# Inputs laid out by copies in a two-layer trunk kernel: x also transposed, weights in streaming order, state tables on their partitions, the scan in contiguous fours

## The chip, the cores and the metric

The kernel runs on one core of one Trainium2 chip. The metric is device time of one execution in microseconds (us), lower is better; the host's work on the inputs is outside it. PE is the matrix engine, DVE the vector engine, ACT the scalar engine, POOL the general one; SP issues most DMAs.

## The reference

Two layers run one after the other on x of 256 positions by 2048 features, fp32. Cut to what matters:

```python
for l in range(2):
    h = rmsnorm(x, pre_norm_g[l])
    q, k, v, z_att, u, z_ssm = split(h @ w_in[l])        # 2048 x 6144, 1024 columns each
    o_att = diff_attention(q, k, v, lam, rel_bias)       # 8 heads, softmax(q1 k1) - lam softmax(q2 k2), masked by chunks of 64
    o_att = rmsnorm(o_att, subln_g[l]) * (1 - lam_init) * silu(z_att)
    y = s5_ssm(u, a, dt, B, C, d)   # 64 groups of 16 channels: h[t] = abar h[t-1] + Bbar u[t], y = Re(C h) + d u
    g_val, g_gate = split(gelu(y) @ w_glu[l])            # 1024 x 2048
    o_ssm = g_val * sigmoid(g_gate) * silu(z_ssm)
    x = x + rmsnorm(concat(o_att, o_ssm) @ w_out[l], post_norm_g[l])   # 2048 x 2048
```

Everything must come out in fp32 accuracy.

## The kernel before, in words

**Halves.** Each layer's weights are cut into 72 chunks of 1 MB, each in two halves of 512 KB: 144 halves a layer, numbered `hs` from 0 (below "half 12" is `hs` = 12, "half 84" is `hs` = 84). A half comes by one DMA from SP's queue into `raw` (128 x 1024, five buffers). ACT copies it to `hi`, rounded to fp32r; DVE makes `lo = raw - hi`; PE multiplies hi by hi, hi by lo and lo by hi and so gets near-fp32 products. In halves 0 to 47 of a layer (U4, u, q, k) that is 24 multiplies of 256 columns; in 48 to 143 (v, za, zs, glu, out) 12 of 512 columns. The first eight halves (U4) fill four accumulators at once, later ones one or two. PSUM has four buffers for accumulators (`acc`) and four for everything else (`side`).

**Order.** The program is written out half by half in the loop over `hs`: DMA for half `hs` + 6, the end of the chunk before (`evac`), `hi` for `hs` + 2, then the other jobs that are due (generators started at fixed halves by `hooks`), `lo` for `hs` + 2, the half's multiplies (`main`), then side jobs that need PE (`run_second`). Each engine takes its own instructions in this order. Long DVE work, as the state scan, is cut into steps and filled in around `lo` by a budget (`fill`, `emit_lo`, constants `BUDS`, `SC`, `CAP`; `cost` is the planned time of a step):

```python
        load[0] += 68 + n / 0.96
            bal = min(bal, CAP) + (BUDL if not l and s >= 44 else BUDS[l]) + pload[0] - load[0] - 1130
```

**The head.** x is loaded by rows of positions (`load_x`, four column blocks of 512 KB between the first weight halves). `build` turns 128 x 128 pieces over PE (`psx`), then ACT writes `hthi` and DVE `htlo`: the transposed, scaled x in hi and lo parts, two of its 16 k pieces per half. `rstd_gen` sums squares on ACT, DVE makes 1/rms, PE spreads it over partitions (`psr`) and ACT copies it to `rbc`; the accumulators of U4 and u can only be read (`u = ac * rbc`, in `evac`) after that. `params_gen` transposes the state poles and vectors over PE and multiplies out the bias table (`psp`).

**State tables and scan.** `prep_gen` loads B and C of a layer by twelve DMAs whose rows are 16 elements long and transposes C over PE (`psc`, four runs of four); for layer 1 that happens in halves 96 onward of layer 0, beside glu. `s_gen` makes the inputs of the state by products (`pss`) and writes `H` (2 parts x 32 group pairs x 64 blocks of four positions). `scan_ops` then steps over the 62 later blocks, each four DVE instructions on 64 elements with a stride of 64. `y_gen` makes y from H (`psy`, `psz`), applies gelu on ACT and DVE, transposes it (`psg`) and writes `ghi` and `glo`, the inputs of glu, with elements 16 bytes apart. Attention runs per head as `soft_gen` (logits, softmax on ACT) and `pv_gen` (transposes `pwt`, ACT copies `wt`, PE makes `po`), in halves 51 to 90.

## Time and profile before

| | us |
|---|---|
| median of 3 runs | 926.35 (925.54 to 928.47) |
| the profiled execution | 926.7 |
| its span (first to last instruction) | 924.9 |
| PE / DVE / ACT busy in it | 907.7 / 683.5 / 488.1 |

The span is what the trace covers; 1.8 us of the execution lie around it. Busy times of the engines overlap, so they don't add up; PE's matmuls are pipelined, and a start-to-start distance says more of PE's pace than the length of one.

### The profile page before, as it was taken

What the parts mean: (1) busy time and instruction counts of PE and PEld (TensorE: products, weight loads), DVE (VectorE), ACT (ScalarE), POOL (GpSimd) and SP (SyncE); (2) the same over time, 40 slices, a digit from 0 to 9 for tenths busy, and PEclk for the clock granted to TensorE, in tenths of its full rate; (3) what the DMA queues carried; (4) which work ended last, traced back from release to release, by engine and by line L of the source; (5) the groups of instructions that cost most, each with busy time, mean ns of one, the idle gap of its engine ahead of it and who ended that gap; (6) DMA issues with size and microseconds to landing.
All of it is one profiled execution on the core that took longest, in us unless ns stands there. A gap on an engine that the chain in (4) does not pass through costs nothing.

```text
span 924.9 us, 17644 instructions
## 1 busy us (share of the span) xinstructions
PE 907.7 (98%) x6722; PEld 795.1 (86%) x6722; DVE 683.5 (74%) x1606; ACT 488.1 (53%) x881; POOL 17.2 (2%) x26
## 2 busy tenths in 40 slices
PE   9999999999999999999999999999999999999995
PEld 8999999888888788887889999997888788888884
DVE  4898686999995756877877449999966566665564
ACT  6643384455465667444468443335565655644451
POOL 3000000000000000000000000000000000000001
PEclk9999999999999999999999999999999999999998
DMA  9988656855654497576656866965556346665852
GB/s 303 209 231 244 185 165 172 278 158 168 184 155 137 126 232 243 171 249 201 215 173 193 230 175 168 246 187 165 163 156 183 115 137 203 197 210 168 291 183 91
DMA packets 187892, 177.21 MB, mean 192 GB/s; under 512 B 42550, under 2 KB 131184, under 8 KB 186912
## 3 DMA queue, kind: packets, MB, share of 16 engines
q1 hardware_dynamic: 187456, 175.96, 64.3%
q8 instruction: 53, 0.87, 0.4%
q14 instruction: 31, 0.25, 0.1%
q0 software_dynamic: 352, 0.13, 0.1%
HBM read 168.44 MB, written 7.88 MB: 191 GB/s over the span
## 4 chain that ended last, share of the span: by engine, by line
PE 87%; DVE 5%; ACT 3%; DMA 2%; SPq 1%; issue 1%; DVEq 0%; ACTq 0%
PE ac L113 79%; DVE lo L116 2%; DMA xt<-in_x_dram 1%; PE lga L113 1%; PE psy L113 1%; PE pss L113 1%; PE po L113 1%; SPq L496 1%; PE psw L97 1%; PE acu L113 1%; ACT junk L134 1%; DMA raw<-in_w_glu_dram 1%; ACT hi L134 1%; DMA raw<-in_w_in_dram 1%; ACT y L134 0%
## 5 line engine op out<-in xcount | busy, mean ns | idle before, releaser
L134 ACT ACTIVATE hi<-raw 128x1024 fp32r<-128x1024 f32 (+1 forms) x282 | 297.8, 1056 | 357.3 <-PE ac L113 272.2
L116 DVE TENSOR_TENSOR lo<-raw,hi 128x512 fp32r<-128x512 f32 (+1 forms) x401 | 359.8, 901 | 105.5 <-ACT hi L134 104.3
L113 PE MATMUL ac<-hthi,hi 128*128 128x256 f32 x736 | 211.7, 288 | 0.3 <-ACT hi L134 0.3
L113 PE MATMUL ac<-htlo,hi 128*128 128x256 f32 x736 | 209.4, 285 | 0.8 <-DVE htlo L123 0.5
L113 PE MATMUL ac<-hthi,lo 128*128 128x256 f32 x736 | 209.1, 284 | 0.6 <-DVE lo L116 0.5
L113 PE MATMUL ac<-hi,hthi 128*128 128x512 f32 x384 | 154.4, 402 | 0.0
L113 PE MATMUL ac<-lo,hthi 128*128 128x512 f32 x384 | 149.8, 390 | 0.4 <-DVE lo L116 0.4
L113 PE MATMUL ac<-hi,htlo 128*128 128x512 f32 x384 | 150.1, 391 | 0.0
L113 PEld LDWEIGHTS ac<-htlo,hi 128*128 128x128 f32 x736 | 141.8, 193 | 1.7 <-DVE htlo L123 1.7
L113 PEld LDWEIGHTS ac<-hthi,hi 128*128 128x128 f32 x736 | 141.7, 193 | 1.3 <-ACT hi L134 0.5
L113 PEld LDWEIGHTS ac<-hthi,lo 128*128 128x128 f32 x736 | 141.7, 193 | 1.2 <-DVE lo L116 1.2
L113 PE MATMUL ac<-lo,mxhi 128*128 128x512 f32 x228 | 89.0, 390 | 0.7 <-DVE lo L116 0.6
L113 PE MATMUL ac<-hi,mxhi 128*128 128x512 f32 x228 | 89.0, 391 | 0.0
L113 PE MATMUL ac<-hi,mxlo 128*128 128x512 f32 x228 | 88.7, 389 | 0.0
L113 PEld LDWEIGHTS ac<-hi,hthi 128*128 128x128 f32 x384 | 72.1, 188 | 16.1
L113 PEld LDWEIGHTS ac<-hi,htlo 128*128 128x128 f32 x384 | 72.1, 188 | 15.8
L113 PEld LDWEIGHTS ac<-lo,hthi 128*128 128x128 f32 x384 | 72.2, 188 | 14.6 <-DVE lo L116 0.8
L113 PEld LDWEIGHTS ac<-lo,mxhi 128*128 128x128 f32 x228 | 42.8, 188 | 10.3 <-DVE lo L116 1.5
L113 PE MATMUL ac<-hi,ghi 128*128 128x512 f32 x128 | 51.5, 403 | 0.0
L113 PEld LDWEIGHTS ac<-hi,mxlo 128*128 128x128 f32 x228 | 42.8, 188 | 8.9
L113 PE MATMUL ac<-lo,ghi 128*128 128x512 f32 x128 | 50.1, 391 | 0.3 <-DVE lo L116 0.3
L113 PEld LDWEIGHTS ac<-hi,mxhi 128*128 128x128 f32 x228 | 42.8, 188 | 8.9
(206 smaller groups left out, 1154.5 us busy)
## 6 DMA issues: line engine op xcount, KB each, us to landing
raw<-in_w_in_dram SPq DMA_DIRECT2D x191, 512.0 KB, 4.2
raw<-in_w_out_dram SPq DMA_DIRECT2D x64, 512.0 KB, 4.7
raw<-in_w_glu_dram SPq DMA_DIRECT2D x32, 512.0 KB, 4.3
U<-uds SPq DMA_DIRECT2D x48, 64.0 KB, 3.3
xt<-in_x_dram SPq DMA_DIRECT2D x8, 256.0 KB, 7.6
uds<-u SPq DMA_DIRECT2D x4, 512.0 KB, 6.0
pg<-in_post_norm_g_dram SPq DMA_DIRECT2D x2, 1024.0 KB, 7.1
xt<-in_x_dram SPq DMA_DIRECT2D x2, 1024.0 KB, 10.1
```

Of the source, the lines that this page charges most:

```text
L97: P.transpose(o, i, idn)
L113: P.matmul(o, lhsT=l, rhs=r, start=start, stop=stop, skip_group_check=True)
L116: V.tensor_tensor(o, a, b, op=op)
L134: A.activation(out=o, in_=i, func=f, **kw)
L496: SY.dma_start(out=bv[64 * d:64 * d + 64, a, r::2], in_=src[l].rearrange("(m r g) p c -> r g p m c", r=2, g=2)[r, d ^ r])
```

## The change

The host now hands over copies of the inputs in other layouts: `xt`, x transposed (x itself is still read for the residual); `wst`, the weights as 288 blocks of 128 x 1024 in the order in which they stream, so that a half is 128 rows of 4 KB in place of pieces of 512 or 2048 bytes; `vecs`, `poles`, `lams` and `bc`, the vectors, poles and B and C of the states already on the partitions on which the kernel uses them. In the kernel:

- The transposes of x in layer 0, of the poles and vectors, and of C in both layers go (`build0` reads `xT`). In layer 1, x is still transposed. The first two pieces of x^T are issued from ACT, the rest from SP between the weights.
- Squares of x in layer 0 are summed over k by DVE and over partitions by two small products (`psv`); `rstd_gen` starts at half 3, before at 1.
- B and C come by two DMAs of 512 KB.
- The scan takes the 64 blocks as 16 groups of four. H's last index is now 16*i + k (block i of group k). 24 steps of 1024 elements and 60 of 64 replace 248 of 64, in each layer; the 1024-wide ones read and write runs of 16 adjacent elements. `u`, `ghi` and `glo` change their order to match.
- `lo` is no longer cut in two around filled work; the budgets are changed; loads and stores of u move by two or three halves; the scan is put on the list before U's second load.
- A second u chunk gets a side buffer as accumulator; half 0 is written by pieces of k.

```diff
-SC = 70
+SC = 57
...
-CAP = 1500.0
-RES = 0.0
+CAP = 1800.0
...
-        load[0] += 68 + n / 0.96
-        return 68 + n / 0.96
+        load[0] += 147 + n / 0.955
+        return 147 + n / 0.955
...
     def emit_dma(hs):
         if hs >= 2 * NCH:
             return
-        l, seg, b = chunks[hs // 2]
...
-        else:
-            SY.dma_start(out=tv, in_=src)
+        SY.dma_start(out=t, in_=wst[hs])
...
         if (weave and budget > 0) or urgent:
             budget = UB if urgent else budget
-            fill(budget / 3)
-            for p in range(2):
-                c = slice(512 * p, 512 * p + 512)
-                tt(lo[:, c], src[:, c], hf[:, c], ALU.subtract)
-                fill(budget / 3)
+            fill(budget / 2)
+            tt(lo, src, hf, ALU.subtract)
+            fill(budget / 2)
...
         ps = side("psp")
-        tpose(ps[:, 0:128], pt[:, 128:256], ident)
-        tpose(ps[:, 128:192], pt[0:64, 384:512], ident[0:64, 0:64])
-        mm4(ps[0:8, 192:512], bt[0:32, 384:392], bt[0:32, 0:320], True, True)
+        mm4(ps[0:8, 0:320], bt[0:32, 384:392], bt[0:32, 0:320], True, True)
         ps2 = side("psp2")
         mm4(ps2[0:8, 0:64], bt[0:32, 384:392], bt[0:32, 320:384], True, True)
-        tpose(ps2[:, 64:82], bt[0:18, 1408:1536], ident[0:18, 0:18])
...
-        cn = R(cslot, "cn")
         cm = R(4, "cm")
         G.memset(cm, 0.0)
+        for c in range(2):
+            SY.dma_start(out=bt[:, 1024 * c:1024 * c + 1024], in_=bc[l, :, 1024 * c:1024 * c + 1024])
         bv = bt[:, 0:1024].rearrange("p (a m c) -> p a m c", a=2, m=NPAIR)
-        for a, src in enumerate((ssm_b_re, ssm_b_im)):
-            for d in range(2):
-                for r in range(2):
-                    SY.dma_start(out=bv[64 * d:64 * d + 64, a, r::2],
-                                 in_=src[l].rearrange("(m r g) p c -> r g p m c", r=2, g=2)[r, d ^ r])
...
         for a in range(2):
-            for hb in range(2):
-                yield 1
-                ps = side("psc")
-                for j in range(4):
-                    tpose(ps[:, 128 * j:128 * j + 128], cv[:, a, 4 * hb + j], ident)
...
-                    act(cmk[rows, 8 * hb:8 * hb + 8, put], pick, AF.Copy, scale=1.0 if a == 0 else -1.0)
-                    act(ccv[rows, a, 16 * hb:16 * hb + 16].rearrange("p (i r) c -> p i r c", r=2), pick, AF.Copy)
+            for d in range(2):
+                rows = slice(64 * d, 64 * d + 64)
+                put = slice(2 * a + 1, 2 * a + 5, 3) if d else slice(2 * a, 2 * a + 6, 5)
+                act(cmk[rows, :, put], ccv[rows, a].rearrange("p (i r) c -> p i r c", r=2), AF.Copy,
+                    scale=1.0 if a == 0 else -1.0)
...
+    def build0(k):
+        act(S["hthi"][:, k], S["xT"][:, k], AF.Copy, scale=pre_g[0][:, k:k + 1])
+        stt(S["htlo"][:, k], S["xT"][:, k], pre_g[0][:, k:k + 1], S["hthi"].bitcast(F32)[:, k], ALU.mult, ALU.subtract)
+
     def build(l, m):
+        if l == 0:
+            for k in (2 * m, 2 * m + 1):
+                build0(k)
+            return
...
     def rstd_gen(l):
-        xt = S["xt"]
-        for n in range(4):
+        if l == 0:
+
+            X = S["xT"].rearrange("p k c -> p (k c)")
+            sq = R(1, "sq")
+            a, b = sq[:, 0:1024], sq[:, 1024:2048]
+            act(a, X[:, 0:1024], AF.Square)
+            yield
+            for n in range(1, 4):
+                act(b, X[:, 1024 * n:1024 * n + 1024], AF.Square)
+                yield
+                tt(a, a, b, ALU.add)
+            for n in (512, 256):
+                tt(a[:, 0:n], a[:, 0:n], a[:, n:2 * n], ALU.add)
+            yield 1
+            psv = side("psv")
             for t in range(2):
-                j = tmp5("junk")
-                act(j, xt[t][:, 512 * n:512 * n + 512], AF.Square, accum_out=ssx[:, t, n:n + 1])
-            yield
+                mm4(psv[:, 2 * t:2 * t + 2], a[:, 128 * t:128 * t + 128], ones[:, 0:2], True, True)
...
             v = st.tile([128, 2], F32, tag="nv", name="nv")
-            V.tensor_reduce(out=v, in_=ssx, axis=AX.X, op=ALU.add)
+            if l == 0:
+                ts(v, psv[:, 0:4:2], EPS * D, None, ALU.add)
+            else:
+                V.tensor_reduce(out=v, in_=ssx, axis=AX.X, op=ALU.add)
...
-                act(H[:, :, 4 * b0 + r:4 * b0 + 8:2, 1:64], psv[:, :, :, 0:63], AF.Copy)
+                hv = H[:, :, 4 * b0 + r:4 * b0 + 8:2]
+                act(hv[:, :, :, 16:64], psv[:, :, :, 0:48], AF.Copy)
+                act(hv[:, :, :, 1:16], psv[:, :, :, 48:63], AF.Copy)
+        weave.append(scan_ops(l))
...
         H = S["H"]
-        ar = apow[:, 0, 32 * l:32 * l + 32, 3].unsqueeze(1).to_broadcast([128, 2, 32])
-        ai = a4s[:, :, 32 * l:32 * l + 32]
-        for s in range(2, 64):
+        c = slice(32 * l, 32 * l + 32)
+        ar = apow[:, 0, c, 3].unsqueeze(1).unsqueeze(3).to_broadcast([128, 2, 32, 16])
+        ai = a4s[:, :, c].unsqueeze(3).to_broadcast([128, 2, 32, 16])
+        br = a16[:, 0, c].unsqueeze(1).to_broadcast([128, 2, 32])
+        bi = a16[:, 1:3, c]
+        sct = R((3, 8)[l], "sct")
+        T, u = (sct[:, 1024 * i:1024 * i + 1024].rearrange("p (a m k) -> p a m k", a=2, m=32) for i in range(2))
+        h = [H[:, :, :, 16 * i:16 * i + 16] for i in range(4)]
+        prev = h[0]
+        for i in range(1, 4):
+            yield mul(u, prev[:, ::-1], ai)
+            yield mul(T, prev, ar)
+            yield tt(u, u, h[i], ALU.add)
+            yield tt(T, T, u, ALU.add)
+            prev = T
+        V.tensor_copy(h[3][:, :, :, 0], T[:, :, :, 0])
+        yield 140
+        for k in range(1, 16):
             t1 = scp.tile([128, 2, 32], F32, tag="sc1", name="sc1")
             t2 = scp.tile([128, 2, 32], F32, tag="sc2", name="sc2")
-            yield mul(t1, H[:, :, :, s - 1], ar) + SC
-            yield mul(t2, H[:, ::-1, :, s - 1], ai)
-            yield tt(t1, t1, H[:, :, :, s], ALU.add) + SC
-            yield tt(H[:, :, :, s], t1, t2, ALU.add) + SC
+            yield mul(t1, h[3][:, :, :, k - 1], br) + SC
+            yield mul(t2, h[3][:, ::-1, :, k - 1], bi)
+            yield tt(t1, t1, T[:, :, :, k], ALU.add) + SC
+            yield tt(h[3][:, :, :, k], t1, t2, ALU.add) + SC
+        for i in range(3):
+            p, o, n = (h[i - 1], h[i], 16) if i else (h[3][:, :, :, 0:15], h[0][:, :, :, 1:16], 15)
+            yield mul(u[:, :, :, 0:n], p[:, ::-1], ai[:, :, :, 0:n])
+            yield mul(T[:, :, :, 0:n], p, ar[:, :, :, 0:n])
+            yield tt(o, o, u[:, :, :, 0:n], ALU.add)
+            yield tt(o, o, T[:, :, :, 0:n], ALU.add)
         S[f"h{l}"] = True
...
-        hv = S["ghi"].rearrange("p (b c i) -> p i b c", b=8, i=4)[:, :, 2 * j:2 * j + 2]
-        lv = S["glo"].rearrange("p (b c i) -> p i b c", b=8, i=4)[:, :, 2 * j:2 * j + 2]
...
+        hv, lv = (S[n].rearrange("p (b k e i) -> p b e i k", b=8, e=4, i=4) for n in ("ghi", "glo"))
+        yv = pg.rearrange("p (i b e k) -> p b e i k", i=4, b=2, e=4)
+        for b in range(2):
+            act(hv[:, 2 * j + b], yv[:, b], AF.Copy)
+        for b in range(2):
+            tt(lv[:, 2 * j + b], yv[:, b], hv.bitcast(F32)[:, 2 * j + b], ALU.subtract)
...
-                S["acc"] = [side("acu") if i % LAYER == 4 else acc("ac")]
+                S["acc"] = [side("acu") if i % LAYER in (4, 5) else acc("ac")]
...
     def hooks(l, s):
-        if s == 1:
+        if s == (1 if l else 3):
...
-            u_store(0 if s == 11 else 4)
-        if s in (12, 18):
-            u_load(0 if s == 12 else 4)
+        if s in (14, 19):
+            u_store(0 if s == 14 else 4)
...
     cur = [0]
-    BUDS = (2250.0, 2200.0)
-    BUDL = 2140.0
+    SPARE = (150.0, 200.0, 300.0)
+    LOT = 1225.0
...
+
+        def load_w0(p):
...
+        load_params()
+        raw[0] = wp.tile([128, 1024], F32, tag="raw", name="raw")
+        load_w0(0)
+        load_x(A, 0, 1)
+        load_x(A, 1, 2)
+        load_w0(1)
         act(cf[:, 0, 0:2], ones[:, 0:2], AF.Tanh)
-        load_params()
-        load_x(0)
-        emit_dma(0)
         emit_dma(1)
-        load_x(1)
+        load_x(SY, 2, 4)
...
-        load_x(3)
-        warm(6)
-        ps = side("psg")
-        P.transpose(ps[:, 0:32], S["pt"][0:32, 0:128], ident[0:32, 0:32])
-        act(prm[:, 0:32], ps[:, 0:32], AF.Copy)
-        warm(W1)
+        load_x(SY, 8, 12)
+        warm(W0)
         at(PG, params_gen())
-        at(2, prep_gen(0, (3, (1, 7), (4, 8))))
...
-                build(l, 0)
-                if not l:
-                    emit_hi(0, True)
-                    emit_lo(0, 0, True)
+                if l:
+                    build(l, 0)
+                else:
+                    for k in range(2):
+                        build0(k)
+                        emit_hi(0, True, (k,))
+                        emit_lo(0, 0, True, (k,))
+                    main(0, part=0)
+                    emit_hi(1)
+                    emit_lo(1, 0)
                 build(l, 1)
...
-            bal = min(bal, CAP) + (BUDL if not l and s >= 44 else BUDS[l]) + pload[0] - load[0] - 1130
+            bal = min(bal, CAP) + (2880.0 if s < 48 else 2724.0) - SPARE[2 if l else int(s >= 44)] + pload[0] - load[0] - LOT
             load[0] = 0.0
-            emit_lo(hs + 2, 0 if s >= SX else min(bal, EB) if s < F0 else bal - RES)
-            bal -= max(0.0, load[0] - 1130)
+            emit_lo(hs + 2, 0 if s >= SX else bal)
+            bal -= max(0.0, load[0] - LOT)
             held = hs in late or 2 * LAYER - LB <= hs < 2 * LAYER
-            main(hs, 0 if held else None)
+            main(hs, 0 if held else None, None if hs else 1)
             pload[0] = 0.0
             run_second()
```

DVE at the start, before: from the first `htlo` to half 2's `lo`. `prm` holds the scales, `psx` transposed x; the two 512-wide `lo` are half 0, the first 1024-wide one half 1.

```order
L123 SCALAR_TENSOR_TENSOR htlo<-psx,prm,hthi 128x256 [waits Activation_49] x2
L116 TENSOR_TENSOR lo<-raw,hi 128x512 [waits DMAHW3_49,Activation_49]
L116 TENSOR_TENSOR lo<-raw,hi 128x512 [waits DMAHW4_49,Activation_49]
L123 SCALAR_TENSOR_TENSOR htlo<-psx,prm,hthi 128x256 [waits PE_49,Activation_49]
L123 SCALAR_TENSOR_TENSOR htlo<-psx,prm,hthi 128x256
L116 TENSOR_TENSOR lo<-raw,hi 128x1024 [waits DMAHW5_49,Activation_49]
L116 TENSOR_TENSOR lo<-raw,hi 128x1024 [waits DMAHW0_49,Activation_49]
```

DVE at the same place after the change; k pieces 0 and 1 are the first two `htlo`, 2 and 3 the next two.

```order
L146 SCALAR_TENSOR_TENSOR htlo<-xT,prm,hthi 128x256 [waits DMAHW2_49,DMAHW0_49,Activation_49]
L139 TENSOR_TENSOR lo<-raw,hi 128x512 [waits DMAHW1_49,Activation_49]
L146 SCALAR_TENSOR_TENSOR htlo<-xT,prm,hthi 128x256 [waits DMAHW4_49,Activation_49]
L139 TENSOR_TENSOR lo<-raw,hi 128x512 [waits DMAHW3_49,Activation_49]
L139 TENSOR_TENSOR lo<-raw,hi 128x1024 [waits DMAHW5_49,Activation_49]
L146 SCALAR_TENSOR_TENSOR htlo<-xT,prm,hthi 128x256 [waits DMAHW6_49,Activation_49]
L146 SCALAR_TENSOR_TENSOR htlo<-xT,prm,hthi 128x256 [waits Activation_49]
L139 TENSOR_TENSOR lo<-raw,hi 128x1024 [waits DMAHW7_49,Activation_49]
```

Half 1's `lo` stood behind the `htlo` of k = 2 and 3 and now stands ahead of them.

PE around `psr` of layer 0, before: `ac_212` is the last of the four accumulators of U4, `acu` a later chunk in a side buffer, its first multiply at half 8.

```order
L113 MATMUL ac_212<-hthi,hi 128x256
L113 MATMUL ac_212<-htlo,hi 128x256
L113 MATMUL ac_212<-hthi,lo 128x256
L113 MATMUL psr<-dg,ones 128x256 [waits DVE_49,PE_49]
L113 MATMUL acu<-hthi,hi 128x256 [waits PE_49,Activation_49]
L113 MATMUL acu<-htlo,hi 128x256
L113 MATMUL acu<-hthi,lo 128x256
```

PE around `psr` after the change; the first `ac` is the first multiply of half 12.

```order
L136 MATMUL acu<-hthi,hi 128x256
L136 MATMUL acu<-htlo,hi 128x256
L136 MATMUL acu<-hthi,lo 128x256
L136 MATMUL psr<-dg,ones 128x256 [waits DVE_49]
L136 MATMUL ac<-hthi,hi 128x256 [waits DVE_49,Activation_49]
L136 MATMUL ac<-htlo,hi 128x256
L136 MATMUL ac<-hthi,lo 128x256
```

`psr` moved from half 8 to just ahead of half 12, and the multiply behind it now waits for DVE, too, because its accumulator takes the buffer of U4's first.

DVE after the change around half 12: `acu` are the two chunks in side buffers, `ac_176` to `ac_179` U4's accumulators.

```order
L139 TENSOR_TENSOR lo<-raw,hi 128x1024 [waits DMAHW1_49,PE_49,Activation_49]
L146 SCALAR_TENSOR_TENSOR pt<-pt 128x64 [waits DVE_49]
L139 TENSOR_TENSOR u<-acu,rbc 128x16x4x4 [waits Activation_49]
L139 TENSOR_TENSOR u<-acu,rbc 128x16x4x4
L139 TENSOR_TENSOR u<-ac_176,rbc 128x16x4x4
L139 TENSOR_TENSOR u<-ac_177,rbc 128x16x4x4
L139 TENSOR_TENSOR u<-ac_178,rbc 128x16x4x4
L139 TENSOR_TENSOR u<-ac_179,rbc 128x16x4x4
L139 TENSOR_TENSOR lo<-raw,hi 128x1024 [waits DMAHW2_49,Activation_49]
```

The two `u` of the side accumulators stand ahead of `ac_176`, the one whose buffer is reused.

ACT before, from the end of half 82 (the softmax's exponentials, `att`) through half 83 (`hi`, then sums of squares `junk` and the `wt` that `po` of half 84 takes).

```order
L134 ACTIVATE att,sm<-att,mx 128x128 [waits DVE_49]
L134 ACTIVATE att,sm<-att,mx 128x256 [waits DVE_49]
L134 ACTIVATE att,sm<-att,mx 128x128 [waits DVE_49]
L134 ACTIVATE att,sm<-att,mx 128x256 [waits DVE_49]
L134 ACTIVATE hi<-raw 128x1024 [waits DMAHW0_49,PE_49]
L134 ACTIVATE junk,as<-po 128x128 [waits PE_49]
L134 ACTIVATE junk,as<-po 128x128 [waits Activation_49]
L134 ACTIVATE wt<-pwt 128x384 [waits PE_49,Activation_49]
```

ACT in half 83 after the change, from `hi` to `wt`; `y` is gelu's tanh for the states.

```order
L157 ACTIVATE hi<-raw 128x1024 [waits DMAHW5_49,DVE_49,PE_49]
L157 ACTIVATE y<-y 128x512 [waits DVE_49]
L157 ACTIVATE junk,as<-po 128x128 [waits PE_49]
L157 ACTIVATE junk,as<-po 128x128
L157 ACTIVATE att,sm<-att,mx 128x128 [waits DVE_49]
L157 ACTIVATE att,sm<-att,mx 128x256 [waits DVE_49]
L157 ACTIVATE att,sm<-att,mx 128x128 [waits DVE_49]
L157 ACTIVATE att,sm<-att,mx 128x256 [waits DVE_49]
L157 ACTIVATE wt<-pwt 128x384 [waits PE_49,Activation_49]
```

The gelu step of `y_gen` now falls into these halves, the exponentials stand in half 83, and `wt` is the last of the half's nine instructions, before of its four.

## Rows read from the trace of the kernel before

**Rows 1.** Part 1 of the page: busy us (share of span), instructions

```profile
PE 907.7 (98%) x6722; PEld 795.1 (86%) x6722; DVE 683.5 (74%) x1606; ACT 488.1 (53%) x881; POOL 17.2 (2%) x26
```

**Rows 2.** Windows: us; PE, PEld, DVE, ACT, POOL busy; clock, DMA, GB/s

```profile
575.00:600.00 25.00, 25.00 (x210) 25.00 (x209) 24.05 (x80) 9.55 (x9) 0.00 (x0) 1.00 0.95 243
```

**Rows 3.** Waits of PE: line, operand, waited-for; us in total, times, longest

```profile
PE ac L113 <- DVE lo L116: 1.9, 5, 0.6
...
PE po L113 <- ACT wt L134: 1.0, 1, 1.0
```

**Rows 4.** Timeline of PE: start, length, instruction, tile, [idle before, releaser]

```profile
7.33 0.39 PE L113 MATMUL ac<-hthi,hi 128*128 128x256 f32 x1 [0.30 <-ACT hi L134]
...
15.12 0.36 PE L113 MATMUL ac<-hthi,hi 128*128 128x256 f32 x1
...
18.59 0.81 PE L113 MATMUL psp<-bt 32*8 32x320 f32 x4
...
50.75 0.36 PE L113 MATMUL ac<-hthi,hi 128*128 128x256 f32 x1
```

**Rows 5.** Windows of the head, 2 to 5 and 5 to 9 us

```profile
2.00:5.00 3.00, 3.00 (x15) 2.65 (x13) 0.00 (x0) 0.42 (x3) 3.00 (x7) 1.00 0.71 221
...
5.00:9.00 4.00, 3.39 (x24) 2.61 (x23) 2.57 (x6) 2.60 (x6) 2.71 (x6) 1.00 0.94 302
```

**Rows 6.** Timeline of DVE and ACT, 8.5 to 11 us

```profile
8.55 0.88 DVE L123 SCALAR_TENSOR_TENSOR htlo<-psx,prm,hthi 128x256 fp32r<-128x256 f32 x2
...
9.65 1.06 ACT L134 ACTIVATE hi<-raw 128x1024 fp32r<-128x1024 f32 x1 [1.13 <-DMA raw<-in_w_in_dram]
...
10.75 1.23 DVE L116 TENSOR_TENSOR lo<-raw,hi 128x1024 fp32r<-128x1024 f32 x1 [1.31 <-ACT hi L134]
```

**Rows 7.** Timeline around `psr` of layer 1, 496 to 501 us

```profile
496.16 0.60 PE L113 MATMUL psr<-dg,ones 128*128 128x256 f32 x2
...
496.41 0.47 PE L113 MATMUL ac<-hthi,hi 128*128 128x256 f32 x1
...
497.52 0.38 ACT L134 ACTIVATE rbc<-psr 128x256 f32<-128x256 f32 x1
...
500.03 2.04 DVE L116 TENSOR_TENSOR u<-ac,rbc 128x256 f32<-128x256 f32 x4
```

**Rows 8.** Timeline of SP, PE and ACT during layer 1's preparation

```profile
326.32 4.68 SPq L496 DMA_DIRECT2D bt<-in_ssm_b_re_dram  x4
...
339.32 0.63 PE L97 MATMUL psc<-ident,cn 128*128 128x128 f32 x4 [0.19 <-DMA cn<-in_ssm_c_re_dram]
...
339.78 0.38 PE L97 MATMUL psf<-ident,za 128*128 128x128 f32 x2
...
343.10 1.06 ACT L134 ACTIVATE hi<-raw 128x1024 fp32r<-128x1024 f32 x1 [3.95 <-DMA raw<-in_w_glu_dram]
```

**Rows 9.** Timeline of PE in glu (346) and out (428)

```profile
346.73 0.48 PE L113 MATMUL ac<-hi,ghi 128*128 128x512 f32 x1
...
347.56 0.50 PE L113 MATMUL ac<-lo,ghi 128*128 128x512 f32 x1 [0.35 <-DVE lo L116]
...
428.94 0.40 PE L113 MATMUL ac<-hi,mxhi 128*128 128x512 f32 x1
...
429.95 0.50 PE L113 MATMUL ac<-lo,mxhi 128*128 128x512 f32 x1 [0.61 <-DVE lo L116]
```

**Rows 10.** Groups by form, DVE: busy us, mean ns, idle before, releaser

```profile
L116 DVE TENSOR_TENSOR sc<-H,apow 128x64 f32<-128x64 f32 x124 | 34.0, 274 | 2.8
...
L116 DVE TENSOR_TENSOR gc<-bt,apow 128x1024 f32<-128x1024 f32 x8 | 9.8, 1220 | 0.0
...
L116 DVE TENSOR_TENSOR glo<-psg,ghi 128x512 fp32r<-128x512 f32 x8 | 8.7, 1090 | 5.2 <-ACT ghi L134 4.8
```

**Rows 11.** Timeline of PE at layer 1's start, and the window 469 to 474

```profile
468.44 0.87 PE L97 MATMUL psx<-ident,xt 128*128 128x128 f32 x6 [1.49 <-DVE xt L123]
...
469.00:474.00 5.00, 4.85 (x26) 4.41 (x25) 3.68 (x7) 3.69 (x9) 0.00 (x0) 0.66 0.34 109
```

254 lines of the change are left out of this document (130 added, 124 removed).

## The prediction

> **What bounds the kernel now.** I read the busy times first: PE is busy for 907.7 of 924.9 us, DVE 683.5, ACT 488.1 [rows 1]. PE busy is no proof of a bound, so I looked for a stretch in which PE does nothing but its main multiplies: from 575 to 600 us it starts 210 of them in 25 us, one per 0.119 us, at full clock, while DVE is busy for 24.05 us [rows 2]. At that pace a half of 24 multiplies takes 2.88 us, and PE never waits there although DVE is full. Next came the waits of PE over the whole run: two of the largest groups are 1.9 us in 5 waits on DVE's `lo` and 1.0 us for one `wt` of ACT [rows 3]; they are that small. So the time is the sum of what PE is given to do, with a head in which data are late and a tail of some 10 us after PE. DVE work taken away is worth something only where PE waits for DVE; PE work taken away counts in full.
>
> The head is where most is lost. The first main multiply starts at 7.33, half 2 begins at 15.12, half 12 at 50.75 [rows 4]. Twelve halves at 2.88 are 34.6 us, so 16.2 us of the first 50.75 are something else: waiting for x and weights, transposes of x (`psx`), of the parameters (`psp`, 0.81 us for the four fp32 products alone [rows 4]) and of C (`psc`). Those times are what the change can take from.
>
> **The change, term by term**, against the profiled execution (926.7 us, 1.8 us more than its span; the median of the runs shown is 0.35 us below it).
>
> *Head, halves 0 to 1.* DMA moves 221 GB/s from 2 to 5 us and 302 from 5 to 9 [rows 5]. Before half 1 the old queue holds 16 KB, half of x's first block (512 KB) and two halves of weights (1024 KB): 1.59 MB, which at these rates is through at 8.1 us. ACT could start `hi` of half 1 at 9.65, released by DMA [rows 6]: landing is seen 1.6 us after the bytes. After the change 1.34 MB stand ahead (parameters 26 KB, two k of x^T, 1024 KB): through at 7.2, seen at 8.8. Then `hi` 1.06, and on DVE `lo` 1.23 as at 10.75 [rows 6]; but now `htlo` of k=2 stands behind that `lo` on DVE, where before it stood ahead. One `htlo` is 0.44 (two in 0.88 [rows 6]). That gives 9.9, 11.1, 11.55: half 1's second multiply at 11.6, and half 2 can begin 23 multiplies later, at 14.4. The removed transposes hardly show here, because PE was waiting for the same bytes. If the landing is seen as early as it can be (no delay) half 2 begins at 12.8; if as late as before, at 15.1.
>
> The two k of x^T that go out from ACT's queue are counted in the same stream of bytes. The Trainium skill (DMA: Bandwidth & Descriptors, Issuing engines are not separate DMA queues) says so: whichever engine issues, the same 16 DMA engines do the work. No run here shows two hardware queues in use at once. Were it otherwise, the 0.26 MB would cost nothing, half 1 would start 0.9 us earlier, and the forecast below would be 919.7.
>
> *Head, halves 2 to 12.* Ten halves are 28.8 us. The `psp` products stay, 0.85 with the switch; the six runs of `psx`, the transposes of parameters and four runs of `psc` are gone. The sum of squares now goes over DVE and two tiny products `psv`: for the products 0.5 (nearest row: `psr`, two multiplies in 0.60 [rows 7]); DVE has by then `lo`, two `htlo`, one 1024-wide add and some parameter steps per half, about 3.4 us against PE's 2.88, so I add 0.4 of waiting (between 0 and 1.3). `psr` itself takes PE 0.25, the step to the next multiply [rows 7].
>
> *A new wait at half 12.* `psr` now stands right before half 12, and half 12's accumulator is the buffer of the first U accumulator; there are four. PE therefore waits until DVE has read that buffer, and DVE first does two `u` of the side accumulators. From the start of `psr`: 0.60 until its result, ACT's `rbc` 0.38, three of the `u` steps (four take 2.04, so three 1.55), 0.2 for the handing over: 2.75, of which PE spends 0.25 on `psr` [rows 7]. The wait is 2.5 us. Everything on PE stands behind it. Before, `psr` stood two halves ahead of the buffer's reuse, and no such wait is in the trace. Bounds: 0 (if the buffer were free earlier) and 2.8.
>
> So half 12 begins at 14.4 + 28.8 + 0.85 + 0.9 + 0.25 + 2.5 = 47.7 in place of 50.75: **3.05 us less**.
>
> *Middle of the run, preparation of layer 1.* The four runs of `psc` each delay the next transposes by 0.46 (339.32 to the `psf` at 339.78 [rows 8]): 1.8 less. The first of them waits 0.2 for its DMA [rows 8]. At 326.32 SP starts to issue twelve loads of B and C in 16-element pieces, and glu's weights queue behind them: ACT waits 3.95 us for weights, PE in the end 0.6 for `lo` (346.73 to 347.56, less the usual 0.23) [rows 8, 9]. Two loads of 512 KB take their place, so these waits go: 0.8 less. ACT's 32 copies out of `psc` become eight longer ones; ACT is not what PE waits for there.
>
> *DVE.* The scan had 496 steps of 64 elements at 0.27 us, 133 us; it gets 120 of them and 48 of 1024 elements. The trace has that width with broadcast operands at 1.22 us [rows 10]; 91 us, 42 less. PE waits for DVE only five times, so most of this buys nothing. At 428.94 PE waits 0.8 us for a `lo` that stood behind 1024-wide `gc` steps (1.01 from start to start, less 0.23) [rows 9, 10]. The new filling puts at most two such steps into a half, not three, and that wait goes: 0.8 less. `ghi` and `glo` are written in steps of 64 bytes, before in steps of 16: still strided, 1.09 us per 512 elements [rows 10], no gain taken.
>
> *A new wait at half 84.* With the scan done by half 78 the first `psy` moves from half 86 to 82, among the attention heads. In half 83 ACT now has `hi`, a tanh, `junk`, four exponentials and then `wt`, and `po` of half 84 waits for that `wt`. The nearest row is the one wait of this kind, 1.0 us [rows 3]. Bounds 0 and 1.0; I take 0.7 **more**.
>
> Wider rows of the weights in the rest of the run, H's copies in two pieces, layer 1's boundary and the tail: nothing, since PE does not wait for these, or they stay.
>
> Sum: 926.7 - 3.05 - 1.8 - 0.8 - 0.8 + 0.7 = 920.95 in the profiled execution, **920.6** as the median.
>
> **The rivals.** *The clock falls in the new wait.* At 468.44 PE has idled 1.49 us after some light work, and from 469 to 474 the mean granted clock is 0.66 [rows 11]: with levels of 1.00 and 0.50 that is 3.4 of the five us at 1.2 GHz. The wait at half 12 is longer. 3.4 us at half pace lose what 1.7 us at full pace do, less what PE waits anyway; I take 1.5: 922.1. The Trainium skill (TensorE: Matmul & The Clock Gate, HAM oscillation — how this bites in real kernels) says that gaps in which PE waits bring the slow clock back for the work behind them; here the trace agrees once. Against it: PE works densely until just before the wait. Chance 0.17.
>
> *The new waits do not appear* (bytes seen earlier, buffer free, `wt` in time): half 2 at 13.6, half 12 at 13.6 + 28.8 + 0.85 + 0.5 + 0.25 = 44.0, so 6.75 in place of 3.05, and no 0.7: 926.35 - 6.75 - 1.8 - 0.8 - 0.8 = 916.2. For it: all these waits are worked out, none is in a row. Chance 0.18.
>
> *The change is hidden:* the bytes ahead of half 1 are nearly the same, so it lands no earlier (half 2 at 15.1), the clock falls at half 12 (half 12 at 49.9), and the waits that go at 346 and 428 come back elsewhere: 926.35 - 0.85 - 1.8 + 0.7 = 924.4, to 926 if ACT's copies at 340 us cost as much as before. Chance 0.09.
>
> *Slower:* the 48 wide steps of the scan read pieces of 16 elements out of H. If they ran at the strided price, 2.13 ns an element as in `glo` [rows 10], each would take 2.2 us in place of 1.22. The new filling leaves DVE about 0.2 us of a half's 2.72 free; the scans spread over some 70 halves, which absorbs 14 us of the extra 47. The rest, 33 us, PE waits for `lo`: 953. It decides from about 1.6 us per step. Against it: `gc`, with broadcast operands, runs at 1.22, and inside a piece the elements are adjacent. Chance 0.06.
>
> **From these to the numbers.** The forecast's own case has 0.5 and spans 917.5 to 923.5 by its bounds. With the rival above it and the two below, 913 to 925.5 leaves out the slow case, part of the hidden one and the edge of the good one: some 2 in 10. A change of 0.3%, about what a measurement of this kernel can tell from none, is 2.8 us, so faster means below 923.6. That is nearly all of the main case, of the case without waits, and half of the clock's: 0.76. Between 923.6 and 929.1: half of the clock's case, most of the hidden: 0.16. Slower: 0.08.
>
> **What would show it.** In the new profile: half 1's second multiply near 11.6 with `lo` or `htlo` as the releaser; a PE gap of about 2.5 us after `psr` near 45 us, released by DVE's `u`; half 12 near 47.7; a clock below 1.00 in that slice if the first rival holds; no `psx` in layer 0, no `psc`; no wait near 340 to 347 and 428; a `po` waiting for `wt` near 280; wide scan steps at about 1.22 us. I am wrong if PE's waits on `lo` grow beyond a few us in the scans (wide steps dear), or if half 12 starts before 45 (the buffer's wait was not there).

## The result, and the profile after

The changed kernel takes 934.85 us (934.11 to 935.33, four runs) against 926.9 for the kernel before beside it: a ratio of 1.0085, interval 1.0066 to 1.0104. Slower by 0.85%, where 920.6 was forecast and the range ended at 925.5. The profiled execution has 935.32 us, its span is 933.5.

Part 1 of the page after, as [rows 1]:

```profile
PE 905.4 (97%) x6674; PEld 793.2 (85%) x6674; DVE 665.1 (71%) x1182; ACT 480.6 (51%) x858; POOL 13.7 (1%) x19
```

Every engine is busy for less time than before, and yet the span is 8.6 us longer, so I looked for waits of PE and for a slower clock. The waits of PE after (line, operand, waited-for; us in total, times, longest), as [rows 3]:

```profile
PE pss L136 <- DMA U<-uds: 6.7, 2, 4.9
PE psv L136 <- DVE sq L139: 2.1, 1, 2.1
PE ac L136 <- DVE u L139: 2.1, 1, 2.1
PE ac L136 <- DVE lo L139: 1.6, 4, 0.6
...
PE po L136 <- ACT wt L157: 1.4, 2, 1.0
...
PE pss L136 <- ACT H L157: 1.0, 2, 0.7
```

The first line is new, and it is the largest wait that either kernel has. The second was forecast at 0.4, the third at 2.5. Where they lie shows best in the starts of the halves, taken from the first main multiply of each (layer, half; us from the span's start):

| half | before | after | after less before | what lies between |
|---|---|---|---|---|
| 0, 2 | 15.12 | 14.50 | -0.62 | the first bytes |
| 0, 7 | 33.54 | 30.13 | -3.41 | `psx` and parameters gone |
| 0, 12 | 50.75 | 52.01 | +1.25 | `psv` and a slow clock; the wait at half 12 |
| 0, 73 | 242.76 | 245.61 | +2.85 | 1.0 of the 1.6 lost are `pss` of layer 0, two waits for ACT's copy to H |
| 0, 76 | 251.87 | 256.95 | +5.08 | three waits for `lo` |
| 0, 96 | 324.56 | 329.72 | +5.17 | the heads and y |
| 0, 105 | 353.72 | 356.23 | +2.51 | `psc` and the wait for weights gone |
| 0, 133 | 435.31 | 436.48 | +1.17 | the wait at 428 gone |
| 1, 15 | 520.82 | 520.45 | -0.37 | the slow clock at the layer's start, absent here |
| 1, 18 | 532.02 | 540.83 | +8.81 | layer 1's `pss` |
| 1, 143 | 911.97 | 920.79 | +8.82 | nothing |

Up to half 15 of layer 1 gains and losses cancel. Then three halves lose 9.2 us, which are never given back. SP's timeline there, the kernel after (start, length, line, tile, count):

```profile
517.49 0.56 SPq L677 DMA_DIRECT2D uds<-u  x1
520.00 0.33 SPq L196 DMA_DIRECT2D raw<-in_wst_dram  x1
524.62 3.61 SPq L686 DMA_DIRECT2D U<-uds  x8
```

And PE's timeline, the first 64 products of `pss` of layer 1, which come in two parts:

```profile
528.39 0.29 PE L136 MATMUL pss<-U,wi 64*64 64x64 f32 x2 [4.91 <-DMA U<-uds]
...
530.44 1.98 PE L136 MATMUL pss<-U,wi 64*64 64x64 f32 x62 [1.75 <-DMA U<-uds]
```

u goes out to DRAM at 517.49 and is there 7.1 us later (from issue to landing, in the list of DMA issues of this stretch). Only then does SP issue the eight loads of U, which takes 3.61 us, and they land 2.3 us after their issue (median of the eight). PE was ready for `pss` at 523.5 and gets U whole at 530.4. This is the store that the change moved from half 11 to 14 and the load that it moved from 12 to 15, in both layers. In layer 0 the loads of U are issued by 82 us, `pss` begins at 141.32, and it does not wait for U.

The loss has a second part, the clock. Windows of the kernel after (columns as in [rows 5]; the granted clock is the third number from the right, and of its two levels 1.00 is 2.4 GHz and 0.50 is 1.2 GHz):

```profile
36.00:40.00 4.00, 4.00 (x25) 4.00 (x25) 3.44 (x17) 0.00 (x0) 0.00 (x0) 0.64 0.43 154
...
528.00:532.00 4.00, 1.86 (x61) 1.78 (x63) 0.00 (x0) 0.00 (x0) 0.00 (x0) 0.58 0.74 268
532.00:536.00 4.00, 4.00 (x33) 3.88 (x29) 0.00 (x0) 1.20 (x4) 0.00 (x0) 0.57 0.11 43
...
469.00:474.00 5.00, 4.24 (x32) 3.80 (x33) 4.21 (x10) 3.91 (x9) 0.00 (x0) 1.00 0.19 72
```

Behind the wait for U the clock stands at half for most of 528 to 536, and behind the wait of `psv` for much of 36 to 40. At 469 to 474, where the kernel before ran at 0.66 [rows 11], it is 1.00 this time.

### The profile page after: what moved, and what is told of

The parts are those of the page before. It is cut to its first block, busy times and chain, and to the rows that moved or that the text cites. A ratio compares the mean times of both kernels' runs of the same rounds, so it can differ in the third digit from the quotient of the medians.

```text
span 933.5 us, 16960 instructions
## 1 busy us (share of the span) xinstructions
PE 905.4 (97%) x6674; PEld 793.2 (85%) x6674; DVE 665.1 (71%) x1182; ACT 480.6 (51%) x858; POOL 13.7 (1%) x19
## 4 chain that ended last, share of the span: by engine, by line
PE 89%; DVE 5%; ACT 2%; DMA 2%; issue 1%; SPq 0%; ACTq 0%; DVEq 0%
PE ac L136 78%; PE acu L136 3%; DVE lo L139 1%; PE lga L136 1%; PE psy L136 1%; PE pss L136 1%; PE po L136 1%; DMA uds<-u 1%; DVE H L139 1%; PE psw L120 1%; DMA xT<-in_xt_dram 1%; ACT hi L157 1%; DVE sq L139 1%; ACT y L157 0%; PE pwt L120 0%
## 5 line engine op out<-in xcount | busy, mean ns | idle before, releaser
L139 DVE TENSOR_TENSOR lo<-raw,hi 128x1024 fp32r<-128x1024 f32 (+1 forms) x282 | 342.7, 1218 | 130.5 <-ACT hi L157 129.3
L136 PE MATMUL ac<-hthi,hi 128*128 128x256 f32 x704 | 201.7, 287 | 2.2 <-DVE u L139 2.1
L136 PE MATMUL ac<-htlo,hi 128*128 128x256 f32 x704 | 199.8, 285 | 0.6 <-DVE htlo L146 0.3
L136 PE MATMUL ac<-hthi,lo 128*128 128x256 f32 x704 | 199.3, 284 | 0.2 <-DVE lo L139 0.2
L136 PEld LDWEIGHTS ac<-hthi,hi 128*128 128x128 f32 x704 | 135.3, 193 | 3.8 <-ACT hi L157 2.5
L136 PEld LDWEIGHTS ac<-htlo,hi 128*128 128x128 f32 x704 | 135.4, 193 | 1.3 <-DVE htlo L146 1.2
L136 PEld LDWEIGHTS ac<-hthi,lo 128*128 128x128 f32 x704 | 135.3, 193 | 0.4 <-DVE lo L139 0.4
L136 PE MATMUL ac<-hi,glo 128*128 128x512 f32 x128 | 50.2, 392 | 0.0
```

The lines of the kernel that those rows point to most:

```text
L136: P.matmul(o, lhsT=l, rhs=r, start=start, stop=stop, skip_group_check=True)
L139: V.tensor_tensor(o, a, b, op=op)
```

## The experiments

All kernels build on the kernel after, unless they say before. "Early u" below is the edit of the first run.

**Early u in layer 1.**

```diff
-        if s in (14, 19):
-            u_store(0 if s == 14 else 4)
-        if s in (15, 20):
-            u_load(0 if s == 15 else 4)
+        us = (11, 17) if l else (14, 19)
+        if s in us:
+            u_store(4 * us.index(s))
+        if s - 1 in us:
+            u_load(4 * us.index(s - 1))
...
-        S["u2"] = s >= 22
+        S["u2"] = s >= (20 if l else 22)
```

> The changed kernel with one edit: in layer 1 the stores of u go out at halves 11 and 17 and the loads of U at 12 and 18, as in the kernel before, not at 14, 19, 15, 20. Theory A (the loss sits in the late round trip of u through DRAM in layer 1): PE's two waits of pss on U (5.06 and 1.93 us near 523 and 528) go, and with them the slow clock behind them (15 multiplies at 0.213 for 0.12, 1.4 us): 8.4 us less, 926.5. Rival B (pss would have waited there anyway, for wi or for the copies of H, or the lost time comes from a DVE that is too full): less than 3 us gained, 932 or more.

Measured 926.54 us (924.99 to 930.88, ten runs), ratio 1.0009, interval 0.9995 to 1.0024: theory A's number, and no difference from the kernel before. SP's and PE's timelines of this run:

```profile
513.92 3.60 SPq L686 DMA_DIRECT2D U<-uds  x8
```

```profile
522.33 1.16 PE L136 MATMUL pss<-U,wi 64*64 64x64 f32 x64
```

The loads are issued until 517.5 and land at about 519.8; `pss` comes at 522.33 and finds them. So U has some 2.5 us to spare here. Three halves later are 8.64 us (3 x 2.88): 6.1 us short, an estimate, beside 6.7 measured. The kernel before had as little to spare:

```profile
514.52 4.05 SPq L691 DMA_DIRECT2D U<-uds  x8
```

```profile
523.79 1.16 PE L113 MATMUL pss<-U,wi 64*64 64x64 f32 x64
```

The eighth load goes out at 518.3 and takes 3.2 us to land (median of the eight): some 2.3 us before `pss`. This could be read before the change was built.

**Late u in the kernel before.** The same edit the other way, with `us = (14, 19) if l else (11, 17)`.

> The kernel before with the same edit the other way: in layer 1 u is stored at halves 14 and 19 and U loaded at 15 and 20. Theory A: pss waits some 7 us for U in the old kernel, too, and the clock falls behind it: 926.4 + 8.4 = 934.8. Rival B (the old kernel's wi or scan is later, so that the wait is hidden, or the wait needs the new kernel's DMA traffic): 928 or less.

Measured 935.32 us (934.71 to 937.21, four runs), ratio 1.0092, interval 1.0076 to 1.0107. Its waits of PE:

```profile
PE pss L113 <- DMA U<-uds: 4.7, 2, 3.2
```

With u's stores and loads moved late the old kernel is as slow as the new one; in its profile halves 15 to 17 of layer 1 take 7.8 us more than before. The move is enough to make the loss, and undoing it is enough to take the loss away.

**Squares ready before `psv`.**

```diff
-        if s == (1 if l else 3):
+        if s == (1 if l else 2):
             at(cur[0], rstd_gen(l))
...
                 tt(a[:, 0:n], a[:, 0:n], a[:, n:2 * n], ALU.add)
+            yield
             yield 1
             psv = side("psv")
```

> The changed kernel with the squares of x in layer 0 started at half 2 instead of 3, and psv left at its place, so that DVE's sums are there when psv comes. Theory A (PE waited 2.25 us at 33.4 for sq, and the clock fell because of it: 18 multiplies at 0.213 for 0.12 from 36.2 to 40.2, 1.7 us): 4.0 us less, 930.9. Rival B (the clock falls there without that wait): 2.3 less, 932.6. Rival C (ACT and DVE are so full in halves 2 to 6 that hi, htlo or lo become late): no gain.

Measured 933.0 us (931.19 to 936.82, five runs; the kernel after took 934.11 to 935.33). In its profile, of the fastest run, the wait is gone and the clock holds: half 10 begins at 40.24 against 43.57, 3.3 us earlier. The median moved by 1.9 only, nearer to rival B's 932.6 than to theory A's 930.9. Two of the five runs are at 935.85 and 936.82 with a mean clock of 0.988, against 0.993 to 0.994 in the others; where the clock fell in those two is not recorded. That the squares caused the wait is shown. That the wait caused the slow clock is not: the run with early u alone has the wait, and its profile keeps the clock at 1.00.

What made `psv` wait, in the kernel after (ACT, then DVE):

```profile
32.22 1.06 ACT L157 ACTIVATE sq<-xT 128x1024 f32<-128x1024 f32 x1 [0.80 <-DVE sq L139]
```

```profile
30.91 1.22 DVE L139 TENSOR_TENSOR sq<-sq 128x1024 f32<-128x1024 f32 x1
32.05 1.22 DVE L139 TENSOR_TENSOR lo<-raw,hi 128x1024 fp32r<-128x1024 f32 x1
33.32 2.41 DVE L139 TENSOR_TENSOR sq<-sq 128x1024 f32<-128x1024 f32 x3
```

It is a chain between two engines through one buffer: ACT's last square waits for DVE's add, the next add waits for that square, and the last three adds take 2.41 us after it. PE stands at `psv` from 33.7 to 35.78.

**A side buffer for half 12.**

```diff
-                S["acc"] = [side("acu") if i % LAYER in (4, 5) else acc("ac")]
+                S["acc"] = [side("acu") if i % LAYER in ((4, 5) if l else (4, 5, 6)) else acc("ac")]
```

> The changed kernel with the accumulator of the third u chunk (halves 12 and 13 of layer 0) in a side buffer, so that half 12 has not to wait for the buffer of U4's first accumulator. Theory A (the 2.24 us at 49.6 are that wait): 2.2 less, 932.6. Rival B (psr or the next accumulator, at half 14, waits instead, or the side jobs lack a buffer): no gain.

Measured 933.81 us (930.62 to 934.87, four runs). In the profile half 12 begins 3.12 us after half 11 and not 5.56: the wait is gone and does not come back at half 14. The median gained only 1.0, and the runs overlap those of the kernel after. In the profiled execution half 2 began 1.0 us later (15.50 for 14.50), before anything that the edit touches, and the clock fell longer behind `psv`:

```profile
36.00:40.00 4.00, 3.21 (x15) 3.21 (x16) 3.97 (x15) 0.18 (x1) 0.00 (x0) 0.58 0.55 163
40.00:44.00 4.00, 4.00 (x22) 4.00 (x22) 0.51 (x6) 1.04 (x1) 0.00 (x0) 0.56 0.62 207
```

**PE kept busy at `psv`.** Early u, and ahead of `psv`:

```diff
+            wv = side("wv")
+            for _ in range(10):
+                mm(wv[:, 0:128], ones, ones, True, True)
             psv = side("psv")
```

> The changed kernel with early u in layer 1, and ten dummy multiplies (128 columns of ones, into a side buffer that nothing reads) ahead of psv in layer 0, so that PE is busy while DVE finishes the sums. The wait's time is not saved. Theory A (the clock falls because PE idles 2.2 us there): no multiply at half pace in halves 8 to 10, and 0.7 to 2 us less than the run with early u alone: 925. Rival B (the clock falls at that place for another reason): slow multiplies stay in halves 8 to 10, 926.5 or, with the dummies' own time, more.

Measured 927.32 us (925.01 to 928.39, eleven runs), ratio 0.9995, interval 0.9985 to 1.0005: by the number rival B. Windows of its profile:

```profile
36.00:40.00 4.00, 4.00 (x35) 3.96 (x35) 3.84 (x18) 0.31 (x1) 0.00 (x0) 1.00 0.52 152
...
52.00:56.00 4.00, 4.00 (x25) 4.00 (x24) 1.57 (x5) 0.57 (x1) 0.00 (x0) 0.63 0.37 129
```

The clock holds behind `psv` and falls behind the wait at half 12, where the kernel after kept it. The runs lie in two groups, 925.01 to 926.24 at a mean clock of 0.996 to 0.997 and 927.32 to 928.39 at 0.992 to 0.994. The run with early u alone had three of ten at 930.2 to 930.9 (0.990 to 0.991), which are absent here. That speaks for theory A, but since that run's own profile kept the clock at 1.00 from 36 to 40 with the wait in it, one profile cannot show it: unsettled.

**All three edits** (early u, squares early, side buffer).

> The changed kernel with three edits together: early u in layer 1, squares of x from half 2 on, and the third u chunk's accumulator in a side buffer. Theory A (the waits add up and nothing else is wrong with the change): 926.5 of the run with early u alone, less 3.6 (halves 8 and 9: 3.24 and 1.57 over their pace against 0.90 and 0.45 with the squares early, taken as in the profiles) and less 2.4 (half 12: 2.67 against 0.24): 920.5, about 0.7% below the kernel before. Rival B (a wait that goes comes back at the next place, since the halves behind it arrive earlier than their weights, u or table steps): 924 or more.

Measured 923.46 us (922.65 to 924.85, five runs), ratio 0.9964, interval 0.9952 to 0.9976. Three us above what the edits were to add up to, and between theory A and rival B. From half 2 to half 12 its profile takes 32.05 us, and 36.04 with early u alone: 4.0 less, not 6.0, because some 1.6 of the 6.0 were the slow clock behind `psv`, which the profile with early u alone doesn't have. Besides, half 2 begins 1.2 us later (16.23 for 15.01), and the clock falls at layer 1's start, which costs 1.5; both change from execution to execution, as said below. The waits that went do not come back. The `lo` waits at halves 73 to 75 are all still there; PE's timeline of the kernel after:

```profile
246.59 0.50 PE L136 MATMUL ac<-lo,hthi 128*128 128x512 f32 x1 [0.59 <-DVE lo L139]
...
250.15 0.50 PE L136 MATMUL ac<-lo,hthi 128*128 128x512 f32 x1 [0.55 <-DVE lo L139]
...
253.38 0.50 PE L136 MATMUL ac<-lo,hthi 128*128 128x512 f32 x1 [0.21 <-DVE lo L139]
```

**The same with the old scan and the old filling** (248 steps of 64, `lo` in two pieces, old budgets and costs); of its edit:

```diff
-SC = 57
+SC = 70
...
-            fill(budget / 2)
-            tt(lo, src, hf, ALU.subtract)
-            fill(budget / 2)
+            fill(budget / 3)
+            for p in range(2):
+                c = slice(512 * p, 512 * p + 512)
+                tt(lo[:, c], src[:, c], hf[:, c], ALU.subtract)
+                fill(budget / 3)
...
+        for s in range(2, 64):
             t1 = scp.tile([128, 2, 32], F32, tag="sc1", name="sc1")
             t2 = scp.tile([128, 2, 32], F32, tag="sc2", name="sc2")
+            yield mul(t1, H[:, :, :, s - 1], ar) + SC
```

> The three-edit version above with the scan, the order of u, ghi and glo, and the filling of the kernel before (248 steps of 64 a layer, lo cut in two, old budgets): so the input layout without the scan's change. Theory A (42 us less of DVE work buys nearly nothing because PE seldom waits for DVE; the new scan costs 1.9 us of lo waits near 246 and the old one 0.8 near 428): 919.5 to 921.5, the same as the three-edit version within 1 us. Rival B (the new scan gains by finishing earlier): 2 us or more above it. Rival C (the new scan's wide steps cost more than that): 2 us or more below.

Measured 920.21 us (919.49 to 920.61, five runs), ratio 0.9925, interval 0.9913 to 0.9938. Rival C: the new scan or its filling costs 3.2 us; halves 73 to 75 take 9.10 us here and 11.40 with the three edits alone. The scan's wide steps are not dearer than the 1.22 us of the forecast. Groups by form of the kernel after, as [rows 10]:

```profile
L139 DVE TENSOR_TENSOR H<-H,sct 128x1024 f32<-128x1024 f32 x8 | 9.7, 1218 | 0.0
...
L139 DVE TENSOR_TENSOR sct<-H,apow 128x1024 f32<-128x1024 f32 x6 | 7.3, 1218 | 0.0
```

But DVE's timeline of the kernel after shows what stands around `lo` (`nwh`, `scal` and `a` are the attention's scales, put in as urgent):

```profile
245.32 1.22 DVE L139 TENSOR_TENSOR lo<-raw,hi 128x1024 fp32r<-128x1024 f32 x1
246.46 0.16 DVE L139 TENSOR_TENSOR nwh<-nwh,a 128x8 f32<-128x8 f32 x1
246.54 1.22 DVE L139 TENSOR_TENSOR sct<-H,apow 128x1024 f32<-128x1024 f32 x1
247.67 0.16 DVE L146 SCALAR_TENSOR_TENSOR nwh<-nwh 128x8 f32<-128x8 f32 x1
247.75 1.22 DVE L139 TENSOR_TENSOR H<-H,sct 128x1024 f32<-128x1024 f32 x1
248.88 1.22 DVE L139 TENSOR_TENSOR lo<-raw,hi 128x1024 fp32r<-128x1024 f32 x1
250.02 0.16 DVE L151 TENSOR_SCALAR a<-a 128x8 f32<-128x8 f32 x1
```

As `fill` is written, it takes one step of the urgent chain and then, since any budget is left, a whole step of the scan. With 0.27 us steps that cost little; with 1.22 us ones a half needs two of them, two small ones and `lo`: 3.56 us from `lo` to `lo` (245.32 to 248.88), where PE wants one each 2.72 us.

**The new scan with its filling mended**, on top of the three edits; of its edit:

```diff
-            if not weave or budget <= 0:
+            if not weave or budget <= 0 or urgent:
                 continue
...
-UB = 1500
+UB = 620
...
-            emit_lo(hs + 2, 0 if s >= SX else bal)
+            emit_lo(hs + 2, 0 if s >= SX else min(bal, 640.0) if s < 7 else bal)
```

> The three-edit version (923.5) with its filling mended in two places, the new scan kept: while an urgent chain runs (the attention's scales near 246), no 1024-wide step goes between its steps; and in halves 0 to 6 of a layer the filling is capped at three steps of 64, as before the change capped it. Theory A (not the scan's arithmetic but where its wide steps and the table steps are put makes lo and htlo late: 2.3 us of it at halves 73 to 75, 1.4 at halves 7 to 9): 920, as with the old scan and filling. Rival B (the scan itself, its wide steps or its earlier psy, costs the 3.2 us): 922.5 or more. Rival C (the wide steps that are held back make y late): 924 or more.

Measured 917.85 us (917.47 to 918.89, four runs), ratio 0.99, interval 0.9885 to 0.9916: the fastest of all, 5.6 us below the three edits alone and 2.4 below the old scan. In its profile halves 73 to 75 take 9.10 us (9.11 before the change), where they took 11.40 with the three edits alone, and halves 2 to 11 of layer 0 take 31.20 for 32.05. So not the scan cost time, but the places of its steps. The gain on the old scan is in part the clock's: at layer 1's start the clock fell in that run's profile and not in this one, 1.5 us. Without that half, and without the head up to half 2, this profile is 1.5 us shorter up to the last half. PE's waits in its profile, the largest in the head's first half:

```profile
PE ac L136 <- ACT hi L157: 1.5, 1, 1.5
...
PE po L136 <- ACT wt L157: 1.0, 1, 1.0
PE pss L136 <- ACT H L157: 1.0, 2, 0.7
PE ac L136 <- DVE lo L139: 0.9, 2, 0.7
```

**The streaming order of the weights alone, in the kernel before**, for all halves and then, with `elif hs < 12`, for halves 0 to 11 only.

```diff
+        if hs == 0:
+            for kk in range(2):
+                SY.dma_start(out=t[:, 512 * kk:512 * kk + 512], in_=wst[hs][:, 512 * kk:512 * kk + 512])
         else:
-            SY.dma_start(out=tv, in_=src)
+            SY.dma_start(out=t, in_=wst[hs])
```

> The kernel before with one part of the change alone: the weights come from the copy in streaming order, 4 KB a row; x, tables, scan and budgets as before. Theory A (row width buys nothing, PE does not wait for weights but at the head and near 343): within 0.3% of before, 926 to 927.5. Rival B (wider rows land earlier: the head's second multiply of half 1 at 11.4 and ACT's 3.95 us wait at 343 come forward): 1 to 2 us less.

> The kernel before with the weights in streaming order for halves 1 to 11 of layer 0 alone (half 0 too, in its two pieces), the rest of the weights from the original arrays. It tells where the 2 us lie that the wider rows gave when all halves had them. Theory A (in the head, the only long stretch in which PE waits for bytes): 925.2, as with all. Rival B (in layer 1's preparation near 340, where the short rows of B and C share the queue with the weights, or spread over the run): 927, as before.

Measured 925.18 us (923.75 to 927.71, twelve runs; ratio 0.9979, interval 0.9969 to 0.9988) and 926.84 (925.49 to 930.36, twelve runs; ratio 1.0, interval 0.9987 to 1.0013). The copy gives some 2 us where nothing was forecast, and laid out for the head alone it gives nothing that can be told from the scatter. Where the 2 us lie, stays open. The first kernel's profile is of an execution of 926.88, one of its slowest, and shows none of the gain: half 12 begins later than before (52.44 for 50.75), from there to half 143 of layer 0 both profiles take 411.8 us, and what is gained up to half 114 of layer 1, 1.5 us, lies nearly all between the starts of halves 0 and 1 of that layer, by a clock that did not fall. The clock is not the whole of it: among runs with the same mean clock of 0.996 the medians are 924.95 (eight runs) and 926.75 (twelve of the kernel before). The Trainium skill (DMA: Bandwidth & Descriptors, Specifications) wants 512 bytes or more for a transfer at full rate, and the shortest rows of the weights before were 512 bytes; by that the copy would buy nothing, and here the kernel with it is 0.2% faster, for a reason that no trace here shows; the copy changes the width of the rows and the place of the weights in DRAM at once.

## Why the prediction was wrong

**The step that failed.** The sum has no term for the moves of u's stores and loads, and so puts them at nothing without a reason. They are in the list of changes and in the diff, but not in the sum, and not among the parts that were put at nothing because "PE does not wait for these, or they stay". In layer 1 the loads had some 2.5 us to spare and were moved by three halves, 8.64 us. The two runs that move them, one in each kernel, gain 8.3 and lose 8.2 us (against 934.85, and against 927.14 beside it): 6.7 us of waiting in the profile, and a clock at half behind it. That is the whole distance from same to slower. It is not the whole distance from the forecast, as the last paragraph of this section says.

**The head, by its terms.** Half 1's second multiply was forecast at 11.6, released by `lo` or `htlo`, and came at 11.64; half 2 at 14.4, and came at 14.50. PE and ACT of the kernel after:

```profile
11.64 0.39 PE L136 MATMUL ac<-htlo,hi 128*128 128x256 f32 x1 [0.30 <-DVE htlo L146]
```

```profile
7.95 0.51 ACT L157 ACTIVATE hthi<-xT,prm 128x256 fp32r<-128x256 f32 x1 [2.02 <-DMA xT<-in_xt_dram]
8.36 1.57 ACT L157 ACTIVATE hi<-raw 128x512 fp32r<-128x512 f32 x2
```

From ACT's `hi` on, the chain is the forecast's. What starts it is not, and there the match is luck: half 1's weights, issued at 1.65, land 6.1 us later (list of DMA issues), at 7.75 and not at 8.8. DMA moved more than the 221 and 302 GB/s that the sum took from before:

```profile
2.00:5.00 3.00, 3.00 (x16) 3.00 (x15) 0.00 (x0) 1.59 (x3) 3.00 (x5) 1.00 0.95 311
5.00:9.00 4.00, 4.00 (x31) 4.00 (x30) 1.66 (x3) 1.98 (x5) 0.55 (x1) 1.00 1.01 362
```

The new profile has a second hardware queue at work, which the forecast had no run of, and wider rows; what each did, this run doesn't tell. But ACT waited until 7.95 for the second piece of x^T and then had half 0's second part to do, and so began half 1's `hi` (the second of the two in the last row) at 8.88. The luck shows in the spread, too: four profiles with this head begin half 2 at 14.50, 14.89, 15.01 and 15.50.

From half 2 to half 12, 33.3 us were forecast and 37.5 measured. The wait at half 12 was forecast as 2.5 and is 2.1 in the list of waits; in the run with the side buffer it is gone, which confirms its cause. Wrong was the term for `psv`: 0.4 of waiting, from DVE's load per half. It is 2.1, beyond its bound of 1.3, because the adds are not load that spreads over halves but a chain with ACT. And the first rival, the slow clock, came true in this execution behind that wait, one before the one that it was tied to; it cost about 1.6 us from 36.25 to 40.7 (half 9 began 4.45 us after half 8, a half being 2.88).

**Layer 1's preparation.** Forecast 1.8 for `psc` and 0.8 for the weights; from half 96 to 105 the kernel after takes 2.66 us less. The sum of the two is right, size included; no run separates them.

**The wait at 428.** Forecast 0.8, measured 1.3 from half 128 to 133. But the reason given, the new filling, is not it: with the old scan and filling in the laid-out kernel that stretch takes the same 13.60 us as with the new one (415.81 to 429.41; 422.88 to 436.48). DVE before and then in that run, behind a pair of `mg` that both have there:

```profile
424.06 1.22 DVE L116 TENSOR_TENSOR gc<-bt,apow 128x1024 f32<-128x1024 f32 x1
...
427.54 1.22 DVE L116 TENSOR_TENSOR gc<-gc,ztmp 128x1024 f32<-128x1024 f32 x1
428.68 2.35 DVE L116 TENSOR_TENSOR lo<-raw,hi 128x1024 fp32r<-128x1024 f32 x2
```

```profile
417.72 1.29 DVE L148 SCALAR_TENSOR_TENSOR mg<-ac,pg 128x512 f32<-128x512 f32 x2 [1.84 <-ACT junk L159]
...
419.45 2.35 DVE L141 TENSOR_TENSOR lo<-raw,hi 128x1024 fp32r<-128x1024 f32 x2
```

In the kernel before, three 1024-wide steps of the tables, with a `lo` cut in two among them, stand between the pair (422.33) and those two `lo`; in the run none does, under the same rule of filling. So the size was about right for a wrong reason; what brings the tables' steps to other places stays open.

**Half 84.** Forecast 0.7. PE of the kernel after, just before half 84 (at 287.88):

```profile
287.19 0.94 PE L136 MATMUL po<-v,wt 128*128 128x128 f32 x6 [0.47 <-ACT wt L157]
```

PE waits 0.5 there, and from half 76 to half 96 the loss is 0.1 in all. Right place, no weight.

**DVE.** The step's 1.22 us held (1.218), so the slower rival's mechanism is refuted, but its place, PE waiting for `lo` in the scan, appeared through the filling: 2.2 us from half 73 to 76, not in the sum. (PE waits for DVE eight times in the list of waits before, five of them for `lo`; the prediction says five in all.)

**The range.** It reached to 925.5 because each new wait was bounded; the wait for U was not among them. But with early u the kernel still takes 926.5, 6 us above the forecast and 1 us above the range, so the move of u is not the only fault of the sum. By number that is the "hidden" case, by mechanism it is not. In the profile with early u half 12 begins 0.3 us later than before, where 3.05 earlier was forecast: half 2 came at 15.01 and `psv` waited 2.1, and the clock did not fall there. Then 1.5 us are lost up to half 73, 1.0 of them in the two waits of `pss` for H, which had no term (the run with the old scan, where H's copies are whole, has 0.8 of them, so the copies in two pieces are not the reason), and 2.2 from half 73 to 76 in the waits for `lo`. The rest came as forecast or a little better, and the clock held at layer 1's start, 1.5 us to the good that no term had.

## What to carry to other kernels

When a change moves a transfer, even by one number in the program, work out its slack: take from the trace when it lands and when its reader comes, in each layer apart, and set the move against the difference. A step made wider for fewer instructions changes what a filler by budget does: look at what one step too many costs the engine that waits. And a change that loses on balance can hold a gain: here the same layouts and scan, with three waits and the filling mended, run 1% faster than the kernel before.
